# A hybrid attention block on one core: attention in two rounds over the heads, with the output projection and FFN products inside the second

## The chip, the core and the metric

The kernel runs on one core of a Trainium2 chip. The metric is the device time of one execution in microseconds (us). A core has five engines that the text names: PE (TensorE, matmuls and transpositions), DVE (VectorE) and ACT (ScalarE), which read the results of PE and prepare its operands, POOL (GpSimd), and SP, which issues the DMA transfers in one queue. Each engine works through its own list of instructions in the order of the program; semaphores tie the lists together. Operands lie in SBUF (128 partitions), results of PE in eight PSUM banks.

## What is computed

A decoder layer on one sequence of 1024 tokens and width 1024, in float32. The cut reference:

```
a = rmsnorm(h); q, k, v, u, z = split(a @ w_in)         # q, k, v, u, z: 1024 x 512
attn = dilated_attention(q, k, v)                       # 8 heads of 64, causal, windows
                                                        # (128, 1), (512, 4), (2048, 16), merged
sgu = spatial_gating(u, z)                              # chunks of 128 tokens
mixed = concat(rmsnorm(attn), rmsnorm(sgu)) @ w_out
h = h + rmsnorm(mixed)
f = rmsnorm(h)
g, up = split(f @ w_gate_up)                            # each 1024 x 2816
h = h + rmsnorm((silu(g) * up) @ w_down)
h = h + sigmoid(h @ w_pe_gate + b) * (p @ w_pe_proj)
```

## The kernel before

**Numbers.** Every large product is made of three matmuls (`mm3`): each operand is split (`split`) into a high half, which ACT casts, and a low half, which DVE subtracts; hi*hi, hi*lo and lo*hi are summed in a PSUM bank. A product of two matrices of 2 x 2 blocks is done as seven block products q = 1 to 7 instead of eight, in `ORDER` (1, 2, 6, 5, 7, 3, 4); the token side of these blocks is held, split, in a `Feat`. `Feat.first` takes the normed tiles 0 to 3 (128 tokens each), transposes them and `put`s blocks 1 and 2; `Feat.second` takes tiles 4 to 7 and forms the other five. Each `put` is two ACT copies and two DVE subtractions of 128 x 256.

**Stages.** The input product (v, then u and z, then q and k), attention, the output projection, the FFN and the gated embedding. Attention goes over four pairs of heads, `attention(pr)`. Each pair has five steps for each of its two heads: step 0 and 1 treat the first half of the queries, "far" the dilated blocks, 2 and 3 the second half; `merge` joins the parts. A step is a chain: score matmuls, a softmax on DVE and ACT, transpositions on PE, a split by ACT and DVE, products with v on PE, and a transposition back. `prepare(pr)` splits q and k of a pair and stacks their halves with nine copies from SBUF to SBUF, each from or to 64 partitions. Between the steps `feed` takes work from `others`, which does not hang on attention: `ple` (the products with `w_pe_proj`) and `gated` (the part of the output projection that takes `sgu`).

Behind attention, `rows_out(t)` does for a tile of 128 tokens the attention part of the output projection (`attn_out`) and the norms (`h_chain`); the normed tile goes to `F.first` or `F.second`. Between the calls of `F.second` the generator `ahead` is fed: `first_products(n)` does, for one of the 22 tiles n of the FFN's width, the two of the seven products (q = 1, 2) that need the first four tiles of tokens only. `gate_up(n)` does the rest of tile n, or all seven products. In the kernel before, `first_products` runs for n = 0 to 6, its results lie in SBUF.

**Order.** The program is recorded as a graph of operations (`Graph`), and `order()` sets the order of each engine by list scheduling: an operation's rank is its place in the recorded program, a ready operation of lower rank goes first, and an engine looks 80 (PE), 40 (DVE, ACT) or 12 (SP) waiting operations ahead. Tiles come from pools, `CAP`: 47 of 4 KB a partition (names m), 14 of 2 KB (s), 28 small ones (t) and the 8 PSUM banks (p); d is DRAM, c a constant. `limits` bounds some groups further: two PSUM banks for fillers ("fill"), three for scores, two for products with v ("av"). All instructions are issued by one line, L382 (L383 in the changed kernel), so that operations are told apart by their tiles.

## Time and profile before

| | us |
|---|---|
| median of three runs | 1205.39 (1204.2 to 1206.11) |
| the profiled execution | 1206.22 |
| its span, first to last instruction | 1204.4 |
| PE busy | 1179.1 (98%) |
| DVE busy | 840.7 (70%) |
| ACT busy | 585.6 (49%) |
| POOL busy | 82.4 (7%) |

The span is the time from the first to the last instruction; the profiled execution's time is a little longer. Busy times of one engine are summed over its instructions. The stages in this execution: the input products last until 226 us, attention from 226 to 461 (its last pair, with rows_out of the first four tiles, from 368), rows_out and the feature tiles of the FFN to 513, the first products to 608, `gate_up` to 894, and then the down product and the embedding.

### The profile page before, as it was taken

The numbers are of one execution on the slowest core, as the hardware profiler recorded it, in microseconds if no ns is written. First come the engines' busy times: TensorE is split into PE (matmuls) and PEld (weight loads), VectorE is DVE, ScalarE is ACT, GpSimd is POOL, SyncE is SP. The second block draws the span as 40 slices with busy tenths as digits, with TensorE's granted clock in tenths as the row PEclk, the third lists the DMA queues.
The fourth block names the chain that finished last, engine by engine and source line by source line (L and its number), as shares of the span: only waits on it lengthen the run. The fifth ranks groups of instructions, "written<-read, shape, count | busy, mean of one in ns | idle before, by whom it ended". The sixth has DMA issues, their size and how long they took to land.

```text
span 1204.4 us, 15994 instructions
## 1 busy us (share of the span) xinstructions
PE 1179.1 (98%) x5633; PEld 983.8 (82%) x5633; DVE 840.7 (70%) x1652; ACT 585.6 (49%) x1262; POOL 82.4 (7%) x124
## 2 busy tenths in 40 slices
PE   8999999999999999899999999999999999999998
PEld 6788888798888777788888888888888888888887
DVE  6888893278646889999865666656567965468643
ACT  7653333399868767632233333333344445357121
POOL 3101010001100244000000000000000000005000
PEclk9999999999999999999999999999999999999999
DMA  8224131859715245315433233233298323753111
GB/s 287 72 79 138 37 127 45 188 174 276 187 39 176 71 140 165 98 53 182 160 111 100 97 125 115 69 121 123 97 333 295 97 96 99 230 178 140 44 44 53
DMA packets 124554, 158.40 MB, mean 132 GB/s; under 512 B 9838, under 2 KB 72634, under 8 KB 124475
## 3 DMA queue, kind: packets, MB, share of 16 engines
q1 hardware_dynamic: 124474, 157.39, 41.0%
q8 instruction: 44, 0.72, 0.3%
q14 instruction: 36, 0.29, 0.1%
HBM read 108.83 MB, written 39.09 MB: 123 GB/s over the span
## 4 chain that ended last, share of the span: by engine, by line
PE 89%; ACT 4%; DVE 3%; POOL 1%; DMA 1%; issue 1%; SPq 0%; DVEq 0%; ACTq 0%; POOLq 0%
PE p L382 89%; ACT m L382 2%; ACT s L382 2%; DVE m L382 2%; POOL t L382 1%; DVE s L382 1%; DVE t L382 1%; DMA m<-in_x 0%; DMA m<-m 0%; SPq L382 0%; ACT t L382 0%; DVEq L382 0%; DVE c L382 0%; ACTq L382 0%; POOLq L382 0%
## 5 line engine op out<-in xcount | busy, mean ns | idle before, releaser
L382 PE MATMUL p<-m,m 128*128 128x512 f32 (+3 forms) x4620 | 1070.0, 390 | 12.4 <-DVE m L382 5.5
L382 PEld LDWEIGHTS p<-m,m 128*128 128x128 f32 x4620 | 861.7, 191 | 184.2 <-DVE m L382 7.2
L382 DVE TENSOR_TENSOR m<-m,m 128x512 fp32r<-128x512 f32 (+2 forms) x473 | 316.6, 704 | 97.7 <-ACT m L382 87.3
L382 ACT CAST m<-m 128x512 fp32r<-128x512 f32 x371 | 219.4, 624 | 246.4 <-PE p L382 158.1
L382 DVE TENSOR_TENSOR s<-p,s 128x512 f32<-128x512 f32 (+4 forms) x159 | 100.8, 642 | 112.5 <-PE p L382 69.5
L382 ACT COPY s<-p 128x512 f32<-128x512 f32 (+1 forms) x139 | 77.0, 557 | 82.4 <-PE p L382 78.9
L382 ACT ACTIVATE s<-s 128x512 f32<-128x512 f32 (+1 forms) x53 | 32.7, 623 | 128.7 <-DVE s L382 128.2
L382 DVE TENSOR_TENSOR m<-p,m 128x256 fp32r<-128x256 f32 (+3 forms) x141 | 67.0, 504 | 38.1 <-PE p L382 26.5
L382 POOL TENSOR_SCALAR t<-t 128x1 f32<-128x1 f32 (+1 forms) x56 | 22.4, 401 | 1009.4 <-ACT m L382 819.7
L382 ACT COPY m<-p 128x512 f32<-128x512 f32 (+1 forms) x85 | 38.7, 473 | 45.6 <-PE p L382 44.4
L382 ACT CAST m<-s 128x256 fp32r<-128x256 f32 (+1 forms) x105 | 47.3, 492 | 26.6 <-PE p L382 16.6
L382 DVE TENSOR_TENSOR m<-s,m 128x256 fp32r<-128x256 f32 (+1 forms) x105 | 51.9, 523 | 5.7 <-ACT m L382 5.7
L382 DVE TENSOR_TENSOR s<-s,s 128x512 f32<-128x512 f32 x75 | 51.1, 690 | 2.6 <-ACT s L382 0.7
L382 PE MATMUL p<-c,m 128*128 128x128 f32 x328 | 48.3, 274 | 0.7 <-DVE s L382 0.4
L382 ACT ACTIVATE m<-m 128x1024 f32<-128x1024 f32 (+2 forms) x45 | 42.5, 945 | 13.3 <-DVE m L382 8.5
L382 POOL TENSOR_TENSOR t<-t,c 128x1 f32<-128x1 f32 (+1 forms) x56 | 45.0, 804 | 4.7
L382 DVE TENSOR_TENSOR s<-p,m 128x512 f32<-128x512 f32 (+1 forms) x32 | 21.6, 674 | 33.5 <-PE p L382 33.1
L382 PE MATMUL p<-c,s 128*128 128x128 f32 (+2 forms) x249 | 42.1, 284 | 3.0 <-DVE s L382 2.8
L382 PEld LDWEIGHTS p<-c,m 128*128 128x128 f32 x328 | 38.0, 140 | 5.9 <-DVE s L382 1.0
L382 DVE CUSTOM_DVE_ANT_0 m<-p,m 128x384 f32<-128x384 f32 (+2 forms) x64 | 30.8, 502 | 15.5 <-PE p L382 15.4
L382 PEld LDWEIGHTS p<-c,s 128*128 128x128 f32 (+2 forms) x249 | 30.9, 146 | 12.4 <-DVE s L382 5.5
L382 ACT CAST s<-p 128x512 fp32r<-128x512 f32 (+2 forms) x64 | 32.5, 532 | 14.0 <-PE p L382 13.8
(58 smaller groups left out, 589.4 us busy)
## 6 DMA issues: line engine op xcount, KB each, us to landing
m<-d SPq DMA_DIRECT2D x55, 512.0 KB, 4.3
d<-s SPq DMA_DIRECT2D x104, 256.0 KB, 2.1
m<-in_w_gate_up SPq DMA_DIRECT2D x88, 256.0 KB, 4.1
m<-in_w_down SPq DMA_DIRECT2D x44, 256.0 KB, 6.1
m<-in_w_in SPq DMA_DIRECT2D x20, 512.0 KB, 4.6
m<-m SPq DMA_DIRECT2D x36, 256.0 KB, 5.0
m<-in_x SPq DMA_DIRECT2D x16, 512.0 KB, 6.0
s<-d SPq DMA_DIRECT2D x16, 256.0 KB, 5.1
```

Source lines behind the costliest of these rows:

```text
L382: getattr(getattr(nc, o.engine), o.what)(*[real(v) for v in o.args], **{k: real(v) for k, v in o.kw.items()})
```

## The change

q and k are kept in halves: the first halves (`qk_low`) stay in SBUF, the second halves, and k's first, are stored to DRAM as they are made (`qd`, `kd`). Attention runs in two rounds over the four pairs. Round one, `first_half`, does steps 0 and 1 of a pair; round two, `second_half`, does "far", 2, 3 and the merge, with q and k loaded again (`prepare_high`). v is loaded in halves, its split first half goes to DRAM in round one and comes back in round two; the biases are loaded once in each round. As the first 512 queries are complete after round one, `rows_out(0)` to `rows_out(3)` and `F.first` run inside round two's first pair, and `first_products` is a filler from then on. It runs for 20 tiles n instead of 7, and its results go to DRAM (`ed`) and are loaded again in `gate_up`. `Feat.second` forms a block and puts it, one after the other, in the order 6, 5, 7, 3, 4, with three small tiles instead of five. `order()` returns the operations in the order in which it picked them.

```diff
-        return sorted(ops, key=lambda o: (o.start, o.i))
+        return picked
...
-        def second(self, t, halves):
+        def second(self, t, halves, order=(6, 5, 7, 3, 4)):
...
-            ps = transposed(halves[0], 4)
-            copy(x3, ps)
-            tt(s3, x1, ps, SUB)
+            copy(x3, transposed(halves[0], 4))
             ps = transposed(halves[1], 4)
-            self.put(4, t, ps)
             tt(s1, ps, x3)
             tt(s2, s1, x1, SUB)
-            tt(s4, x2, s2, SUB)
-            for q, v in ((5, s1), (6, s2), (3, s4), (7, s3)):
-                self.put(q, t, v)
+            for q in order:
+                if q == 7:
+                    tt(x3, x1, x3, SUB)
+                if q == 3:
+                    tt(s2, x2, s2, SUB)
+                self.put(q, t, {6: s2, 5: s1, 7: x3, 3: s2, 4: ps}[q])
...
-    qf, kf = [M() for _ in range(4)], [M() for _ in range(4)]
+    qk_low, qk_high = [M(F32, (P, 2, 512)) for _ in range(4)], [M(F32, (P, 2, 512)) for _ in range(4)]
+    qd, kd = DR([AW, 512]), DR([AW, S])
...
+            if q in (3, 7, 4):
+                load({3: kd[rs, LO], 7: kd[rs, HI], 4: qd[rs]}[q], dst)
...
+    def stacked(q, k):
...
+        both, ql = M(F32R, (P, 2, 512)), SM(F32R)
+        qh, q1 = both[:, 0], both[:, 1]
...
+            split(kh[:, cs], kl[:, cs], v)
+        load(q1[bot].f32(), qh[bot].f32(), 0.6)
+        load(q1[top].f32(), ql[bot].f32(), 0.6)
+        load(qh[bot].f32(), ql[top].f32(), 0.6)
         for dst, src in ((k1, kh), (l1, kl)):
...
+            load(dst[bot].f32(), src[bot].f32(), 0.6)
+            load(dst[top].f32(), src[bot].f32(), 0.6)
+        load(kh[bot].f32(), kh[top].f32(), 0.6)
+        load(kl[bot].f32(), kl[top].f32(), 0.6)
+        return (qh, kh, kl), (q1, k1, l1)
+
+    def prepare_low(pr):
+        low = qk_low[pr]
+        qk[pr] = stacked(low[:, 0], [low[:, 1]])
+
+    def prepare_high(pr):
+        rs = slice(pr * P, (pr + 1) * P)
+        q, k = SM(), M()
+        load(q, qd[rs])
+        load(k, kd[rs])
+        qk[pr] = stacked(q, [k[:, LO], k[:, HI]])
...
+    EARLY = 20
+    FB, FH, FF2, FA, FO = 36, 0, 48, 60, 100
+    TODO = (((0, "far"), ("h", 0)), ((0, "far"), ("h", 1)), ((0, 2), ("h", 2)), ((0, 2), ("h", 3)), ((0, 3), ("f", 0)),
+            ((0, 3), ("f", 1)), ((0, 3), ("f", 2)), ((0, 3), ("f", 3)))
+    ed = {n: DR([2 * P, 512]) for n in range(EARLY)}
...
     def first_products(n):
 
-        both = M(F32, (P, 2, 512)) if n < 5 else None
-        p1, gate0 = early[n] = (both[:, 0], both[:, 1]) if both else (SM(), SM())
-        raw = M(F32, (P, 8, P), "raw")
+        p1, gate0, raw = SM(), SM(), M(F32, (P, 8, P), "raw")
...
         copy(p1, ps)
+        load(ed[n][:P], p1)
...
         tt(gate0, ps, p1)
+        load(ed[n][P:], gate0)
+        early.add(n)
...
     def gate_up(n):
...
-            (u, gate0), one, p1 = early.pop(n), PB(), None
-            p1, u = u, SM()
+            one, u, gate0, p1 = PB(), SM(), SM(), SM()
+            load(p1, ed[n][:P])
+            load(gate0, ed[n][P:])
...
+    def first_half(pr, fills, then):
+        v, b, vs, both = load_v(pr, slice(0, 512)), M(F32, (P, 2, 512)), [], M(F32R, (P, 8, P))
+        load(b, a["c_bias"][2 * pr : 2 * pr + 2, :, :512].rearrange("h p c -> p h c"))
         for hh in range(2):
...
+            v_halves(vhl, v, hh)
+            load(vcd[pr][hh].then(lambda u: u.rearrange("(j p) d -> p j d", p=P)), vhl.f32())
+            vs.append({j: vhl[:, j, :] for j in range(4)})
+        for step in (0, 1):
+            for hh in range(2):
+                unit(pr, hh, step, vs[hh], b[:, hh])
+                fed(fills, (0.15, 0.35)[step])
+            if step in then:
+                then[step]()
+
+    def second_half(pr, fills, then):
+        v, v3, vs, biases = load_v(pr, slice(512, S)), SM(F32R, (P, 2, P)), [], []
+        for hh in range(2):
+            b, vhl = M()[:, :896], M(F32R, (P, 8, P))
             load(b, a["c_bias"][2 * pr + hh])
+            load(vhl[:, :4, :].f32(), vcd[pr][hh].then(lambda u: u.rearrange("(s c) d -> s c d", c=4)))
+            load(v3[:, hh, :].f32(), vcd[pr][hh][384:512])
+            v_halves(vhl[:, 4:, :], v, hh)
...
-        for step in (0, 1, "far", 2, 3):
+        for step in ("far", 2, 3):
...
+                fed(fills, {"far": 0.15, 2: 0.12, 3: 0.23}[step])
...
-    prepare(0)
-    for pr in range(3):
-        attention(pr, [(others, (40, 60, 110)[pr])], {1: lambda: prepare(pr + 1)})
-    attention(3, [(others, 104)], {"far": lambda: rows_out(0, 1), 2: lambda: rows_out(2, 3)})
+    prepare_low(0)
+    for pr in range(4):
+        nxt = (lambda: prepare_low(pr + 1)) if pr < 3 else (lambda: prepare_high(0))
+        first_half(pr, [(others, FA)], {0: nxt})
+    ahead = chain(*(first_products(n) for n in range(EARLY)))
...
+    for pr in range(4):
+        then = {}
+        for step in ("far", 2, 3):
+            def hook(pr=pr, step=step):
+                for name, t in todo.get((pr, step), ()):
+                    if name == "h":
+                        rows_out(t)
+                    else:
+                        F.first(t, halves_of(t))
+                        if t == 3:
+                            fills.append((ahead, FB))
+                if step == 2 and pr < 3:
+                    prepare_high(pr + 1)
+            then[step] = hook
+        second_half(pr, fills, then)
     run(others)
-    ahead = chain(*(first_products(n) for n in range(7)))
-    for t in range(4):
-        rows_out(t + 4)
-        F.first(t, halves_of(t))
-    feed(ahead, 24)
     for t in range(4, NT):
-        feed(ahead, 24)
+        feed(ahead, FH)
+        rows_out(t)
+    for t in range(4, NT):
+        feed(ahead, FF2)
         F.second(t, halves_of(t))
     run(ahead)
```

How it moves instructions, at three places. First PE, where the products of q and k end. Before, the last product (q = 4, the split weights m_1988) is followed by transpositions and products of `ple` (c_73 is the identity, s_1772 a tile of p):

```order
L382 MATMUL p_1551<-m_527,m_1988 128x512
L382 MATMUL p_1551<-m_547,m_1988 128x512
L382 MATMUL p_1551<-m_527,m_1988 128x512
L382 MATMUL p_2158<-c_73,s_1772 128x128 x2
L382 MATMUL p_2161<-c_73,s_1859 128x128 x2
L382 MATMUL p_2173<-c_73,s_1990 128x128 x2
L382 MATMUL p_2178<-m_1835,s_2168 128x512
L382 MATMUL p_2178<-m_1897,s_2168 128x512
```

In the changed kernel the same product (weights m_2005) is followed by the first scores (m_2101 and m_2110 hold the stacked k of two heads, m_1773 their q):

```order
L383 MATMUL p_1565<-m_561,m_2005 128x512
L383 MATMUL p_1565<-m_577,m_2005 128x512
L383 MATMUL p_1565<-m_561,m_2005 128x512
L383 MATMUL p_2197<-m_2101,m_1773 128x128
L383 MATMUL p_2199<-m_2101,m_1773 128x256
L383 MATMUL p_2202<-c_73,s_1790 128x128 x2
L383 MATMUL p_2206<-m_2110,m_1773 128x128 x2
L383 MATMUL p_2209<-c_73,s_1830 128x128 x2
L383 MATMUL p_2217<-m_2110,m_1773 128x256 x2
L383 MATMUL p_2197<-m_2101,m_1773 128x128
```

The scores of the first pair have moved up to the last product, and the transpositions of `ple` stand between them.

Second DVE, near the end of `F.second`. Before (the `put`s have 128x2x128; the 128x512 rows with two m tiles as sources are splits of FFN weights):

```order
L382 TENSOR_TENSOR s_5725<-m_5199,s_5710 128x512
L382 TENSOR_TENSOR m_5468<-s_5700,m_5456 128x2x128
L382 TENSOR_TENSOR m_5475<-s_5700,m_5461 128x2x128
L382 TENSOR_TENSOR m_5481<-s_5710,m_5464 128x2x128
L382 TENSOR_TENSOR m_5489<-s_5710,m_5470 128x2x128
L382 TENSOR_TENSOR m_5507<-s_5725,m_5473 128x2x128
L382 TENSOR_TENSOR m_5519<-s_5725,m_5479 128x2x128
L382 TENSOR_TENSOR m_5527<-s_5673,m_5431 128x2x128
L382 TENSOR_TENSOR m_5541<-s_5673,m_5437 128x2x128
L382 TENSOR_TENSOR m_5533<-m_5386,m_5533 128x512
L382 TENSOR_TENSOR m_5646<-m_5386,m_5646 128x512
```

And in the changed kernel:

```order
L383 TENSOR_TENSOR m_6008<-s_5908,m_5992 128x2x128
L383 TENSOR_TENSOR m_6013<-s_5908,m_5995 128x2x128
L383 TENSOR_TENSOR s_5939<-m_4177,s_5939 128x512
L383 TENSOR_TENSOR m_5898<-m_5786,m_5898 128x512
L383 TENSOR_TENSOR m_5982<-m_5850,m_5982 128x512
L383 TENSOR_TENSOR m_6041<-s_5939,m_6029 128x2x128
L383 TENSOR_TENSOR s_6046<-p_6010,s_6015 128x512
L383 TENSOR_TENSOR m_6006<-m_5850,m_6006 128x512
L383 TENSOR_TENSOR s_6066<-p_6048,s_6051 128x512
L383 TENSOR_TENSOR m_6071<-s_5939,m_6033 128x2x128
```

The run of eight `put` subtractions ahead of a split is gone; splits stand between the `put`s.

Third SP, in `gate_up`. Before, loads of raw weights (m from in_w_gate_up) and stores of results (d from s or m):

```order
L382 DMA d_98<-m_5449 128x512
L382 DMA m_6131<-in_w_gate_up 128x4x128 x2
L382 DMA d_99<-m_5554 128x512
L382 DMA d_100<-s_6220 128x512
L382 DMA d_101<-s_6235 128x512
L382 DMA d_102<-s_6120 128x512
L382 DMA d_103<-s_6253 128x512
L382 DMA m_6267<-in_w_gate_up 128x4x128
```

In the changed kernel, at a similar place, with the first products' results coming back (s from d_102, d_103):

```order
L383 DMA m_6454<-in_w_gate_up 128x4x128 x2
L383 DMA m_6461<-in_w_gate_up 128x4x128 x2
L383 DMA s_6474<-d_102 128x512
L383 DMA d_119<-s_6471 128x512
L383 DMA s_6483<-d_102 128x512
L383 DMA d_119<-s_6500 128x512
L383 DMA m_6570<-in_w_gate_up 128x4x128 x2
L383 DMA m_6579<-in_w_gate_up 128x4x128 x2
L383 DMA s_6592<-d_103 128x512
L383 DMA d_120<-s_6081 128x512
```

Between the weight loads stand the reloads of `ed`, each 128x512.

## Rows read from the trace of the kernel before

**Rows 1.** The page, part 1: busy us (share of the span) and instructions of each engine.

```profile
PE 1179.1 (98%) x5633; PEld 983.8 (82%) x5633; DVE 840.7 (70%) x1652; ACT 585.6 (49%) x1262; POOL 82.4 (7%) x124
```

**Rows 2.** Table by stretches; its first line names the columns, x counts instructions.

```profile
core 0: us, PE busy (x) PEld busy (x) DVE busy (x) ACT busy (x) POOL busy (x), PEclk, DMA share, GB/s
226.00:247.00 21.00, 18.07 (x93) 15.49 (x92) 8.83 (x35) 13.38 (x34) 0.00 (x0) 0.92 0.88 233
247.00:368.00 121.00, 120.85 (x751) 105.78 (x749) 79.09 (x261) 100.89 (x282) 6.83 (x16) 1.00 0.61 173
368.00:461.00 93.00, 87.27 (x500) 73.13 (x499) 79.62 (x194) 72.55 (x197) 25.06 (x41) 1.00 0.36 116
461.00:513.00 52.00, 48.17 (x221) 39.45 (x220) 47.19 (x91) 33.85 (x79) 9.81 (x11) 0.97 0.46 132
513.00:608.00 95.00, 95.00 (x420) 78.69 (x420) 85.51 (x134) 28.50 (x47) 0.00 (x0) 1.00 0.43 136
608.00:894.00 286.00, 286.00 (x1263) 236.89 (x1262) 170.41 (x262) 101.45 (x180) 0.00 (x0) 1.00 0.36 119
```

**Rows 3.** Timeline of PE, 225 to 247 us: start, length, instruction xcount [idle before <-releaser].

```profile
226.12 0.81 PE L382 MATMUL p<-c,s 128*128 128x128 f32 x6
...
234.71 2.39 PE L382 MATMUL p<-m,m 128*128 128x128 f32 x8 [2.57 <-DMA m<-m]
...
242.48 0.82 PE L382 MATMUL p<-c,m 128*128 128x128 f32 x6
...
246.03 0.66 PE L382 MATMUL p<-s,m 128*128 128x256 f32 x4
```

**Rows 4.** PE by form in the four stretches, in turn: xcount | busy, mean ns | idle before.

```profile
L382 PE MATMUL p<-m,s 128*128 128x512 f32 x30 | 8.1, 426 | 0.4 <-ACT s L382 0.4
...
L382 PE MATMUL p<-m,m 128*128 128x512 f32 x6 | 2.3, 476 | 0.0
...
L382 PE MATMUL p<-m,m 128*128 128x512 f32 x190 | 55.5, 411 | 0.0
...
L382 PE MATMUL p<-m,s 128*128 128x512 f32 x66 | 21.6, 421 | 0.0
...
L382 PE MATMUL p<-m,m 128*128 128x512 f32 x203 | 51.3, 398 | 3.0 <-ACT m L382 2.6 <-DVE t L382 0.2
...
L382 PE MATMUL p<-m,m 128*128 128x512 f32 x189 | 46.2, 403 | 3.8 <-DVE m L382 3.8
```

**Rows 5.** Waits of PE, 226 to 513 us: releaser, us in total, times, longest us.

```profile
PE p L382 <- DVE m L382: 3.8, 1, 3.8
PE p L382 <- ACT m L382: 2.6, 2, 1.4
PE p L382 <- DMA m<-m: 2.6, 1, 2.6
```

**Rows 6.** Timeline of PE, 496 to 517 us.

```profile
506.99 10.31 PE L382 MATMUL p<-m,m 128*128 128x512 f32 x37 [3.83 <-DVE m L382]
```

**Rows 7.** Timeline of DVE, 503 to 509 us.

```profile
503.57 2.77 DVE L382 TENSOR_TENSOR m<-s,m 128x256 fp32r<-128x256 f32 x8
506.25 1.89 DVE L382 TENSOR_TENSOR m<-m,m 128x512 fp32r<-128x512 f32 x3
...
508.17 0.69 DVE L382 TENSOR_TENSOR m<-m 128x512 f32<-128x512 f32 x1
```

**Rows 8.** Timeline of SP's issues, 214 to 240 us.

```profile
214.76 15.76 SPq L382 DMA_DIRECT2D m<-m  x14
```

**Rows 9.** DMA issues by kind: xcount, KB each, median us from issue to landing.

```profile
d<-s SPq DMA_DIRECT2D x104, 256.0 KB, 2.1
m<-in_w_gate_up SPq DMA_DIRECT2D x88, 256.0 KB, 4.1
...
m<-m SPq DMA_DIRECT2D x36, 256.0 KB, 5.0
...
s<-d SPq DMA_DIRECT2D x16, 256.0 KB, 5.1
```

**Rows 10.** DVE by form, 226 to 513 us: xcount | busy, mean ns | idle before, releaser.

```profile
L382 DVE TENSOR_TENSOR s<-p,s 128x512 fp32r<-128x512 f32 x32 | 22.0, 689 | 17.8 <-ACT s L382 17.5
```

More of the change, by code (lines that the diff above doesn't have):

```diff
@@ L246, in order @@
         coming, events = [], [0.0]
-        done, first = [False] * n, 0
+        done, first, picked = [False] * n, 0, []
         def release(o):
@@ L321, in order @@
                 o.start, o.engine = now, e
+                picked.append(o)
                 if o.table and o.table != table:
@@ L630, in x_chain @@
             norm_apply(v, xt[:, cs], rstd, g_pre[:, cs])
-        (A.first if t < 4 else A.second)(t, xn)
+        (A.first if t < 4 else A.second)(t, xn, *([(4, 5, 6, 3, 7)] if t >= 4 else []))
     def v_out(t, terms):
@@ L886, in far_unit @@
         oT = SM()
-        copy(oT.then(lambda v: v.rearrange("p (s c) -> p c s", c=4)), po)
-        turn_back(oT, far[pr][:, :, hh * HD : (hh + 1) * HD], 4)
+        copy(oT.split(4), po.then(lambda v: v.rearrange("p c s -> p s c")))
+        turn_back(lambda ii: oT[:, ii * P : (ii + 1) * P], far[pr][:, :, hh * HD : (hh + 1) * HD], 4)
     def merge(pr):
@@ L993, in h_chain @@
         kept[t] = m
-    raws, early, y_even = {}, {}, []
+    raws, early, y_even = {}, set(), []
     def halves_of(t):
@@ L1086, in feed, with v_halves, load_v @@
             n -= got
-    def attention(pr, fills, then):
-        v = M(F32, (P, 8, P))
-        load(v, vd[:, pr * P : (pr + 1) * P].then(lambda x: x.rearrange("(j p) c -> p j c", p=P)))
-        biases, vhls = [], []
-        for hh in range(2):
-            b = M()[:, :896]
+    vcd = [[DR([512, P]) for _ in range(2)] for _ in range(4)]
+    def v_halves(dst, v, hh):
+        split(dst[:, :, 0:HD], dst[:, :, HD:], v[:, :, hh * HD : (hh + 1) * HD])
+    def load_v(pr, rs):
+        v = SM(F32, (P, 4, P))
+        load(v, vd[rs, pr * P : (pr + 1) * P].then(lambda x: x.rearrange("(j p) c -> p j c", p=P)))
+        return v
@@ new lines, in fed @@
+    def fed(fills, share):
+        for fill, n in fills:
+            feed(fill, n * share)
+    def first_half(pr, fills, then):
+        v, b, vs, both = load_v(pr, slice(0, 512)), M(F32, (P, 2, 512)), [], M(F32R, (P, 8, P))
+        load(b, a["c_bias"][2 * pr : 2 * pr + 2, :, :512].rearrange("h p c -> p h c"))
+        for hh in range(2):
+            vhl = both[:, 4 * hh : 4 * hh + 4, :]
+            v_halves(vhl, v, hh)
[7 more added lines that the diff above has]
+                then[step]()
@@ L1097, in attention @@
-            split(vhl[:, :, 0:HD], vhl[:, :, HD:], v[:, :, hh * HD : (hh + 1) * HD])
-            vhls.append(vhl)
-        vcs = []
-        for vhl in vhls:
-            vcd, vc = DR([512, P]), SM(F32R, (P, 4, P))
-            load(vcd.then(lambda u: u.rearrange("(j p) d -> p j d", p=P)), vhl[:, :4, :].f32())
-            load(vc.f32(), vcd.then(lambda u: u.rearrange("(s c) d -> s c d", c=4)))
-            vcs.append(vc)
+            vs.append({3: v3[:, hh, :], "far": vhl[:, :4, :], **{j: vhl[:, j, :] for j in range(4, 8)}})
@@ L1105, in attention @@
         stats[pr], far[pr] = [T1(8) for _ in range(4)], SM(F32, (P, 4, P))
-        for step in (0, 1, "far", 2, 3):
+        for step in ("far", 2, 3):
             for hh in range(2):
                 if step == "far":
-                    far_unit(pr, hh, vcs[hh], biases[hh])
+                    far_unit(pr, hh, vs[hh]["far"], biases[hh])
                 else:
-                    unit(pr, hh, step, vhls[hh], biases[hh])
-                for fill, share in fills:
-                    feed(fill, share * {0: 3, 1: 7, "far": 5, 2: 4, 3: 7}[step] / 52.0)
+                    unit(pr, hh, step, vs[hh], biases[hh])
+                fed(fills, {"far": 0.15, 2: 0.12, 3: 0.23}[step])
```

54 lines of the change are left out of this document (25 added, 29 removed).

## Prediction

> **What bounds the kernel now.** I read the page's busy shares first: TensorE (PE) is busy 98% of the span, VectorE (DVE) 70%, ScalarE (ACT) 49% [rows 1]. PE is the bound, and neither kernel saves it work: the order of the changed kernel holds the same 5601 PE instructions. So the only time to win is time in which PE stands still or steps slowly. The table by stretches tells where that is [rows 2]: from 513 to 894 us PE is busy 95.00 of 95.00 and 286.00 of 286.00 us; the gaps lie between 226 and 513 us, in attention (226 to 461) and in the norms and feature products behind it (461 to 513).
>
> Busy time hides part of it, since PE overlaps its matmuls: a 512-column matmul has a mean of some 400 ns [rows 4], but 1263 of them fill 286.00 us, so one starts every 0.2264 us [rows 2]. Short ones start every 0.11 us (128 columns: 0.82 us for six, (0.82 − 0.27)/5) to 0.12 us (256 columns: (0.66 − 0.30)/3) [rows 3]; I take 0.113 for all of them. Now each stretch gets a floor, its 512-column matmuls [rows 4] by 0.2264 plus the rest by 0.113, and a slack, its length less that floor:
>
> 226 to 247: 36 and 57, floor 14.6, slack 6.4. 247 to 368: 256 and 495, floor 113.9, slack 7.1 (6% of the floor). 368 to 461: 203 and 297, floor 79.5, slack 13.5 (17%). 461 to 513: 189 and 32, floor 46.4, slack 5.6 (12%). Sum: 254.4 of floor, **32.6 us of slack**.
>
> Why it is there: the first stretch has one wait of 2.57 us on the copies that stack q and k, and then a granted clock of 0.92 on average [rows 2, 3, 5]. The two levels being 1 and 1/2, that is (1 − 0.92) × 2 × 21 = 3.4 us at the lower one, 1.7 us lost. The last has one wait of 3.83 us: a split (the subtraction that makes the low half of a weight tile) stands on DVE behind eight `put` subtractions, 2.77 us, of `F.second` [rows 6, 7]; the clock after it costs (1 − 0.97) × 52 = 1.6 us [rows 2]. The two middle ones have many small gaps. What separates 6% from 17% there is load. DVE's busy time against the floor is 79.6/79.5 = 1.00 in 368 to 461 and 47.2/46.4 = 1.02 in 461 to 513, against 79.1/113.9 = 0.69 (ACT 0.89) in 247 to 368; from 513 to 608 it is 85.5/95 = 0.90, and PE does not stop [rows 2]. So gaps grow when DVE's load reaches PE's.
>
> The Trainium skill ("Perfetto Trace Analysis", section Identifying the Most-Contended Engine) says that the busy share of matmuls is not a good measure of the distance to the roof, and that the share of weight loads (LDWEIGHTS) is. The rows bear out the first half: the matmuls leave only 287 − 274.4 = 12.6 us idle in 226 to 513, far less than the slack. The second half decides a rival below.
>
> **The change, part by part.** Nothing is removed from PE. What moves is work that does not hang on attention: 13 more n of `first_products` (n 7 to 19, 24 matmuls each, 312 × 0.2264 = 70.6 us) go from `gate_up` to the stretch around attention, 216 matmuls of n 0 to 8 inside round two, and rows_out and `F.first` of the first four tiles go into round two as well. I cut the changed PE order into stages, counted its matmuls, put DVE's and ACT's instructions of each stage at the durations of the trace, and gave each stage the slack of the nearest row by load:
>
> (a) Start of attention, 143 matmuls (64 long), floor 23.4, load DVE 0.71, ACT 0.91. The low halves of k are done 48 matmuls (10.9 us) before the first score, since q=4 only writes the second half of q. But 16 DMAs stand ahead on SP's queue (the stores of k, the copies of pairs 0 and 1), which now move at 0.5 to 1.13 us each (14 copies took 15.76 us [rows 8]; half as long ones should take half). 16 × 0.65 = 10.4 us: the scores wait for 0 to 2 us. And no `ple` work stands behind q=4 to fill it. I take 3 us, between nothing and the 6.4 of today.
> (b) Rest of round one, 485 (240), floor 82.0, loads 0.54 and 0.76: below those of 247 to 368, so 6% as there, 4.9.
> (c) rows_out 0 to 3 and `F.first` in pair 0, 274 (100), floor 42.3, DVE 0.96, ACT 0.85: nearly the 1.00 of 368 to 461, so 15%, 6.3.
> (d) Pairs 1 to 3 with FFN products, 547 (228), floor 87.7, loads 0.73 and 0.74: 6%, 5.3.
> (e) rows_out 4 to 7, 171 (144), floor 35.7, DVE 0.80: between 0% (at 0.90, 513 to 608) and 17%, I take 8%, 2.9.
> (f) `F.second` with 216 long matmuls of FFN products between its tiles, floor 52.5, DVE 0.89: like 513 to 608, 0.5. Two things take the wait at 503 away: `put` subtractions alternate with the splits in DVE's order, and there are two n of ready products (48 matmuls, 10.9 us) for each tile, against 2.77 us of subtractions.
> (g) `gate_up` of 20 early n. Each of the 13 new ones turns two ACT copies into DVE additions and adds a third: 39 × 0.60 us ((1.89 − 0.69)/2 for a 512-column one [rows 7]) = 23.4 us of DVE, its load there rising from 0.60 to 0.80, below the 0.90 that cost PE nothing. It adds 40 reloads of 256 KB. A reload lands in 5.1 us and a raw weight tile in 4.1 [rows 9], and the order issues them a whole n (60 matmuls, 13.6 us) ahead. I take 1 us.
>
> Floors of (a) to (f) sum to 323.6 = 254.4 + 70.6 less rounding, so no PE work is lost in the count. Slacks: 3 + 4.9 + 6.3 + 5.3 + 2.9 + 0.5 + 1 = 23.9 against 32.6, **a gain of 8.7 us**. The profiled run took 1206.22 us, its span 1204.4; 1206.22 − 8.7 = 1197.5. That run lies 0.83 above the median of 1205.39, so the median should be **1196.7**.
>
> Bounds. (b) and (d) could be at 17% (+9.0, +9.6) or at none (−4.9, −5.3), (a) at 6.4 or 0, (c) at 6 to 17% (−3.7, +0.9), (e) at 0 or 17% (−2.9, +3.2), (f) at up to 5.6 (+5.1), (g) at up to 4 (+3.0). All highs together are not likely: as independent ends their squares sum to a width of 15 up and 9.5 down. Since the loads of (b) and (d) are below that of the 6% row, their upper ends are remote, and I take two thirds of the upward width.
>
> **Rivals.** *Nearly no gap is left:* with FFN products at hand in (c) to (f) PE never starves, as from 513 to 608. Then (c) to (f) fall to some 2 us, (b) to 3, in all 9 to 10 with (a) and (g): 1205.39 − 23 = 1182. Against it: round one has only the same fillers as today, and each product needs a split of its own on the loaded DVE.
>
> *The gaps move along:* they are the latency of score, softmax, transposition, split, product. DVE stands for 17.5 us in 226 to 513 behind ACT's casts in that chain [rows 10], and the change has as many of these chains as before. Slack then stays at some 30: 1203 to 1205, no change.
> Read by the weight loads, as that page has it, there is little to win: 233.85 of 287 us is 81.5% in 226 to 513 against 82.8% in 608 to 894, room for 4.6 us, and some 1201 at best; how far the trace bears this out is weighed in this rival's chance.
>
> *The copies become the bound (slower):* every hand-over of a pair in round two needs nine copies on 64 partitions, six of 1.13 us and three of half of that, 8.5 us of SP's queue, behind two loads from DRAM, with FFN loads and stores in the same queue. Copied bytes rise from 9.4 to 12.6 MB. In the order the last copy of pairs 1 to 3 is issued 42 to 49 PE rows (7 to 9 us) ahead of its use, and a copy lands in 5.0 us [rows 9]. If the queue is late by more than that, each hand-over costs what 231.8 us does today: 2.6 of wait and 1.7 of clock [rows 2, 3], 4.3 us; four of them are 17.2, hence 1196.7 + 17.2 = 1213.9. It decides from (1207.8 − 1196.7)/4 = 2.8 us a hand-over.
> By the skill ("SBUF — State Buffer", Door 1: The DMA port swizzle), transfers on 64 partitions reach half of the ports, some 218 GB/s; fourteen copies in 15.76 us are 233 GB/s [rows 8], which agrees. By that rule, which speaks against this change, 3.1 MB more would be an estimated 14 us of port time; it costs only where PE waits for it.
>
> That the change does not do what it says is excluded: the order shows the two rounds, and the FFN products among them.
>
> **How the numbers follow.** Forecast (gaps partly closed) 0.68, nearly no gap 0.09, gaps move along 0.12, copies 0.11. Range: 1186 (the forecast's lower width of 9.5, and a part of the second case beyond) to 1206 (two thirds of 15 upwards, with most of the no-change case). A measurement can tell about 0.2% (2.4 us) from no change: faster is below 1203.0, slower above 1207.8. Faster takes nearly all of the forecast and the second case: 0.76; same 0.13; slower 0.11.
>
> **What would show it.** Right: the 2.57 and 3.83 us waits of PE are gone, the clock is 1.00 where `F.second` runs, and PE's busy share is near full from the FFN products on. (a) wrong: PE waits for copies at the first scores. (c) wrong: a stretch with rows_out in pair 0 whose DVE is full and whose PE idles by more than 7 us. (g) wrong: PE waits on DVE or on reloads in `gate_up`. The prediction fails if several waits on copies of over 2 us, each with a fall of the clock, appear between pairs of round two, or if DVE bounds two of the stages.

## The result and the profile after

The changed kernel takes 1194.29 us (median, 1191.19 to 1200.4), the kernel before 1205.39: 11 us faster. The ratio, here and below taken from the means of the runs, is 0.9914, with a 95% interval of 0.9891 to 0.9937. The forecast was 1196.7, with a range of 1186 to 1206. The execution that was profiled took 1197.43 us, its span 1195.6; against the 1206.22 us of the profiled execution before that is 8.8 us less (forecast: 8.7). So the sum holds in both ways of counting, but most of its terms do not, and that is where the learning is.

The page, part 1, as in [rows 1]: PE is the bound as before, DVE has 28 us more to do, ACT 15 us less.

```profile
PE 1175.6 (98%) x5633; PEld 981.4 (82%) x5633; DVE 868.5 (73%) x1702; ACT 571.0 (48%) x1248; POOL 83.6 (7%) x125
```

The table by stretches, in the columns of [rows 2], cut at the borders of the stages (a) to (g) of the prediction; (a) begins at 223.40 us, and 348.0 us lie behind (g):

```profile
223.40:247.20 23.80, 23.80 (x145) 20.73 (x144) 17.08 (x52) 22.91 (x61) 0.00 (x0) 1.00 0.99 323
247.20:333.20 86.00, 85.55 (x486) 73.27 (x485) 48.34 (x139) 66.40 (x175) 8.98 (x24) 1.00 0.66 207
333.20:383.70 50.50, 47.04 (x275) 40.34 (x275) 40.84 (x107) 36.65 (x102) 14.77 (x19) 1.00 0.57 165
383.70:485.10 101.40, 97.48 (x548) 83.78 (x549) 65.96 (x200) 67.46 (x192) 0.00 (x0) 0.97 0.71 199
485.10:521.10 36.00, 36.00 (x172) 29.85 (x171) 28.89 (x50) 18.57 (x41) 15.30 (x23) 1.00 0.41 131
521.10:573.60 52.50, 52.50 (x249) 43.90 (x248) 48.29 (x93) 34.05 (x78) 3.40 (x3) 1.00 0.81 259
573.60:847.60 274.00, 272.72 (x1202) 225.07 (x1202) 229.14 (x356) 76.18 (x134) 0.00 (x0) 1.00 0.55 170
```

Taking the prediction's floors from these lengths gives the slack of each stage:

| stage | length | floor | slack forecast | slack measured |
|---|---|---|---|---|
| (a) start of attention | 23.8 | 23.4 | 3 | 0.4 |
| (b) rest of round one | 86.0 | 82.0 | 4.9 | 4.0 |
| (c) pair 0 of round two, rows_out, F.first | 50.5 | 42.3 | 6.3 | 8.2 |
| (d) pairs 1 to 3 with FFN products | 101.4 | 87.7 | 5.3 | 13.7 |
| (e) rows_out 4 to 7 | 36.0 | 35.7 | 2.9 | 0.3 |
| (f) F.second with FFN products | 52.5 | 52.5 | 0.5 | 0.0 |
| (g) gate_up, 20 n | 274.0 | 271.7 | 1 | 2.3 |
| sum | 624.2 | 595.3 | 23.9 | 28.9 |

In whole lengths: 226 to 894 us before [rows 2] was 668.0; two n of `gate_up` (2 x 84 matmuls x 0.2264 = 38.0 us) now lie behind (g), so 630.0 stand against 624.2, 5.8 us won. The part ahead is 2.6 us shorter (226.0 to 223.4), the part behind 0.4 (310.4 to 348.0 − 38.0): 8.8. By the slacks only 32.6 − 28.9 = 3.7 of the 5.8 would be won. The other 2.1 us are in the floors: a row by stretches counts a matmul that lies across a border in both stretches. The counts before hold 7 long and 5 short matmuls more than those of (a) to (g) (2199 against 2192, 881 against 876), though the work is the same, and 7 x 0.2264 + 5 x 0.113 = 2.1 us. Counted once, the slack before is 34.7 us, and 5.8 us of it are won.

PE's waits between 223 and 574 us, as in [rows 5]: the 3.8 us behind the `put`s are gone, and so is the copy at 231.8 us, but another copy is waited for.

```profile
PE p L383 <- DMA m<-m: 2.4, 1, 2.4
PE p L383 <- DVE m L383: 2.2, 2, 1.4
...
```

That one is at the hand-over to the last pair. PE's timeline, and the table by stretches around it:

```profile
446.83 1.06 PE L383 MATMUL p<-m,m 128*128 128x512 f32 x4
450.29 1.19 PE L383 MATMUL p<-m,m 128*128 128x128 f32 x4 [2.40 <-DMA m<-m]
```

```profile
440.00:450.00 10.00, 7.89 (x49) 6.70 (x47) 2.87 (x8) 5.10 (x14) 0.00 (x0) 1.00 1.00 249
450.00:455.00 5.00, 4.71 (x19) 4.41 (x20) 3.96 (x17) 3.14 (x7) 0.00 (x0) 0.77 0.69 228
455.00:460.00 5.00, 5.00 (x24) 4.30 (x23) 2.77 (x13) 3.28 (x14) 0.00 (x0) 0.89 0.05 20
```

The reader is to see three things: PE waits 2.40 us; the DMA engines were busy throughout the 10 us ahead (share 1.00) and yet moved no more than 249 GB/s, where stage (a) moved 323 at 0.99; and the clock fell behind the wait, to 0.77 and 0.89, which costs 0.23 x 5 + 0.11 x 5 = 1.7 us. What fills these 10 us is not the copies. The DMA view of the stretch:

```profile
DMA packets 3327, 2.49 MB, mean 249 GB/s; under 512 B 95, under 2 KB 3001, under 8 KB 3326
...
m<-in_w_gate_up SPq DMA_DIRECT2D x2, 512.0 KB, 9.9
...
m<-m SPq DMA_DIRECT2D x1, 256.0 KB, 10.2
```

One copy of 256 KB is issued there. It lands 10.2 us later, beside two raw weight tiles of 512 KB, and nine of ten packets are under 2 KB. So the copy landed late in a queue full of other transfers, here loads of the FFN products that the change pulled into the stage. That these loads alone make it late is not shown: e4, which has none of them in round two, also waits 1.6 us for a copy at a hand-over. Copies alone are seen before, in the 14 of [rows 8]:

```profile
214.80:230.60 15.80, 15.43 (x71) 12.56 (x70) 4.92 (x9) 5.46 (x12) 0.00 (x0) 1.00 0.92 200
```

The Trainium skill ("SBUF — State Buffer", Door 1: The DMA port swizzle) puts transfers on 64 partitions at half of the ports, some 218 GB/s; this row, 200 GB/s at a share of 0.92, agrees. (The prediction's 233 GB/s divides by the time of issuing, in which the last copies had not yet landed.)

The stage (c) has its waits where DVE and ACT are both full. Two rows of the table by stretches:

```profile
380.00:385.00 5.00, 2.79 (x13) 1.83 (x14) 5.00 (x13) 5.00 (x19) 0.00 (x0) 0.95 1.00 258
385.00:390.00 5.00, 5.00 (x23) 4.25 (x23) 3.23 (x10) 3.25 (x13) 0.00 (x0) 0.71 0.65 227
```

From 380 to 385 us DVE and ACT are busy for 5.00 of 5.00, PE for 2.79; the clock is 0.95 and then 0.71, another 0.25 + 1.45 = 1.7 us, all of it in (d), as the clock is 1.00 to the end of (c) at 383.7 us.

The third place in (d) is a raw weight tile that comes late. ACT, then PE:

```profile
414.89 0.62 ACT L383 CAST m<-m 128x512 fp32r<-128x512 f32 x1 [1.82 <-DMA m<-in_w_gate_up]
```

```profile
415.83 0.44 PE L383 MATMUL p<-c,s 128*128 128x128 f32 x2 [1.40 <-ACT s L383]
```

ACT stands 1.82 us for `m<-in_w_gate_up`; behind it in ACT's list stands a copy for attention, and PE waits 1.40 us for that with a transposition.

### The profile page after: what moved, and what is told of

It is laid out like the page before. It is cut to its first block, busy times and chain, and to the rows that moved or that the text cites. A ratio compares the mean times of both kernels' runs of the same rounds, so it can differ in the third digit from the quotient of the medians.

```text
span 1195.6 us, 16385 instructions
## 1 busy us (share of the span) xinstructions
PE 1175.6 (98%) x5633; PEld 981.4 (82%) x5633; DVE 868.5 (73%) x1702; ACT 571.0 (48%) x1248; POOL 83.6 (7%) x125
## 4 chain that ended last, share of the span: by engine, by line
PE 89%; DVE 3%; DMA 3%; ACT 2%; POOL 1%; issue 1%; SPq 0%; ACTq 0%; DVEq 0%; POOLq 0%
PE p L383 89%; DVE s L383 2%; ACT m L383 2%; POOL t L383 1%; DMA s<-d 1%; DMA m<-m 1%; DVE t L383 1%; DVE m L383 1%; DMA m<-in_w_gate_up 1%; DMA m<-in_w_in 1%; ACT s L383 0%; POOL m L383 0%; SPq L383 0%; ACTq L383 0%; DVEq L383 0%
## 5 line engine op out<-in xcount | busy, mean ns | idle before, releaser
L383 DVE TENSOR_TENSOR s<-p,s 128x512 f32<-128x512 f32 (+4 forms) x218 | 139.3, 653 | 79.6 <-PE p L383 49.6
L383 ACT ACTIVATE s<-s 128x512 f32<-128x512 f32 (+1 forms) x71 | 44.1, 626 | 227.6 <-DVE s L383 171.7
L383 DVE TENSOR_TENSOR m<-p,m 128x256 fp32r<-128x256 f32 (+3 forms) x136 | 63.7, 496 | 44.4 <-PE p L383 23.4
L383 ACT COPY s<-p 128x512 f32<-128x512 f32 (+1 forms) x118 | 59.9, 516 | 47.2 <-PE p L383 46.4
L383 ACT CAST m<-s 128x256 fp32r<-128x256 f32 (+1 forms) x121 | 53.1, 478 | 35.4 <-DMA s<-d 12.5
L383 DVE TENSOR_TENSOR s<-s,s 128x512 f32<-128x512 f32 x88 | 60.7, 692 | 4.4 <-ACT s L383 0.7
L383 ACT ACTIVATE m<-m 128x1024 f32<-128x1024 f32 (+1 forms) x36 | 36.8, 1023 | 31.2 <-DVE m L383 16.9
L383 PE MATMUL p<-s,m 128*128 128x128 f32 (+1 forms) x256 | 45.8, 284 | 0.2 <-PE p L383 0.2
L383 PEld LDWEIGHTS p<-s,m 128*128 128x128 f32 x256 | 39.9, 197 | 4.4 <-ACT m L383 0.4
L383 ACT ACTIVATE m<-m,t 128x384 f32<-128x384 f32 (+2 forms) x64 | 37.1, 583 | 8.6 <-DVE t L383 8.5
```

The source lines that it names most:

```text
L383: getattr(getattr(nc, o.engine), o.what)(*[real(v) for v in o.args], **{k: real(v) for k, v in o.kw.items()})
```

## The experiments

Each is compared with the kernel before on the same chip; the ratio is given with its interval. Two parts were first taken one by one.

**e1: the new F.second alone, in the kernel before** (with the order of picking; F.second also serves the input products, there in the order 4, 5, 6, 3, 7 as in the changed kernel).

```diff
-        def second(self, t, halves):
+        def second(self, t, halves, order=(6, 5, 7, 3, 4)):
...
-        return sorted(ops, key=lambda o: (o.start, o.i))
+        return picked
```

> The kernel before with the new Feat.second alone (a block is formed and put, one after the other; x_chain with its own order 4, 5, 6, 3, 7) and the order of picking; attention in one round, seven n of first products as before. Theory 'puts': the gain is made where PE is 2.6 us earlier at the start of attention (226.0 against 223.4 us) and where the 3.83 us wait behind eight put subtractions went with its clock (5.6 us of slack in 461 to 513 against 0.3 in the two stages of after); two rounds win some 9 us in round one and lose as much in round two. Then this kernel takes 1205.4 - 2.6 - 5 = 1198. Theory 'products at hand': the gain comes from 13 more n to fill gaps, and the start is an accident: 1203 to 1205.

Measured: 1203.42 us, 0.9991 (0.9981 to 1.0002): no difference that can be told. The wait has shrunk by 0.9 us only. DVE and then PE, around 500 us:

```profile
497.60 0.42 DVE L383 TENSOR_TENSOR m<-p,m 128x256 fp32r<-128x256 f32 x1
...
498.60 1.76 DVE L383 TENSOR_TENSOR m<-s,m 128x256 fp32r<-128x256 f32 x5
500.27 1.29 DVE L383 TENSOR_TENSOR s<-m,s 128x512 f32<-128x512 f32 x2
501.48 0.68 DVE L383 TENSOR_TENSOR m<-m,m 128x512 fp32r<-128x512 f32 x1
```

```profile
502.22 58.11 PE L383 MATMUL p<-m,m 128*128 128x512 f32 x248 [2.97 <-DVE m L383]
```

The split (the 128x512 `m<-m,m`) stands behind eight `put` subtractions as before, three from 497.60 us on and the five shown, and behind two sums, and PE waits 2.97 us instead of 3.83. So at this place the `put`s do not alternate with splits; the new F.second does not bring that about by itself. Theory 'puts' falls.

**e2: 20 n of first products through DRAM as well, attention still in one round.**

```diff
-    ahead = chain(*(first_products(n) for n in range(7)))
+    ahead = chain(*(first_products(n) for n in range(EARLY)))
...
-    feed(ahead, 24)
     for t in range(4, NT):
-        feed(ahead, 24)
+        feed(ahead, FF2)
```

> The same, and 20 n of first products through DRAM, 48 matmuls of them ahead of each tile of F.second; attention still in one round. Theory 'puts': the wait is gone already, so no more than 1 us against the kernel with the new puts alone, 1197 to 1199; and as two rounds bring nothing, equal to the changed kernel within 3 us. Theory 'products at hand': as the gaps of 368 to 513 lie where products can't yet help in one round, 1199 to 1202, and the two rounds make the rest.

Measured: 1202.42 us, 0.9986 (0.9977 to 0.9995). The wait in F.second is gone with 48 matmuls between its tiles, but some of it comes back in `gate_up`, where the kernel before has none. PE's waits, 600 to 900 us:

```profile
PE p L383 <- DVE s L383: 2.4, 2, 1.7
```

So products without the two rounds are worth some 1.7 us, less than either theory gave.

**e3: the changed kernel with 7 n of first products.**

```diff
-    EARLY = 20
+    EARLY = 7
```

> The changed kernel with 7 n of first products instead of 20 (through DRAM as there). They are used up in round two's second and third pair and nothing is left for F.second. Theory 'products at hand': F.second starves as before, 4 to 8 us more than the changed kernel, 1199 to 1202. Theory 'puts': the puts alternate with nothing to split, F.second costs PE 2 us at most, and gate_up is rid of 26 reloads: 1192 to 1196.

Measured: 1228.56 us, 1.0194 (1.0169 to 1.0219). Slower than the kernel before by 23 us, and the changed kernel by 34, far beyond either expectation. The seven n are used up, and F.second stands alone. The row for its stretch:

```profile
505.00:536.00 31.00, 8.28 (x38) 6.12 (x37) 29.94 (x57) 18.86 (x50) 10.13 (x9) 0.60 0.56 170
```

DVE is busy 29.94 of 31 us, PE 8.28, and the clock is 0.60.

**e4: the changed kernel without first products in round two** (all 20 n remain, fed from F.second on).

```diff
-    FB, FH, FF2, FA, FO = 36, 0, 48, 60, 100
+    FB, FH, FF2, FA, FO = 0, 0, 48, 60, 100
```

> The changed kernel with no first products inside round two (all are fed from F.second on). Theory 'products at hand': pairs 1 to 3 of round two lose their filler, and 216 matmuls (49 us) of cover with it; slack there grows from 13.7 to 20 or more: 1200 to 1206. Rival 'queue': the slack in round two is made by transfers (at 440 to 450 us the DMA engines are busy 1.00 and PE waits 2.4 us for a stacking copy), and with nine fewer raw loads of 512 KB in the queue the wait goes: 1190 to 1194.

Measured: 1209.43 us, 1.0042 (1.0027 to 1.0057): 5 us slower than before, 15 slower than the changed kernel. The gaps open in round two, and the clock goes with them:

```profile
384.00:410.00 26.00, 21.92 (x126) 18.25 (x124) 22.59 (x76) 23.19 (x76) 0.00 (x0) 0.87 0.76 217
410.00:450.00 40.00, 35.44 (x226) 31.50 (x227) 29.32 (x107) 30.68 (x97) 0.00 (x0) 0.91 0.56 154
```

PE's idle time in these rows, 4.1 and 4.6 us, is only half of the price: the clock takes up to 0.13 x 26 + 0.09 x 40 = 7.0 us more. (From 384 to 450 us the changed kernel has 3.6 us of idle time and 1.7 of clock.) Theory 'products at hand' stands: two rounds without products inside them cost time, products without the two rounds (e2) hardly save any, both together are 10 to 11 us faster.

**e8: 24 matmuls instead of 48 between the tiles of F.second.**

```diff
-    FB, FH, FF2, FA, FO = 36, 0, 48, 60, 100
+    FB, FH, FF2, FA, FO = 36, 0, 24, 60, 100
```

> The changed kernel with 24 instead of 48 matmuls of first products ahead of each tile of F.second (the rest follows behind it). The stage's matmuls shrink from 52.5 to some 31 us, DVE's work there from 48 to some 40: DVE's load goes from 0.9 to 1.3 of PE's. Theory 'load': DVE becomes the bound of the stage, 6 to 10 us more: 1200 to 1205. Rival: it needs only something at hand between the tiles, as the puts alternate with splits: 1194 to 1197.

Measured: 1212.35 us, 1.006 (1.0042 to 1.0077), 17.6 us above the changed kernel (0.0146 x 1205), the sign of theory 'load' with a larger size. The stage, and then PE's wait behind it:

```profile
521.00:541.00 20.00, 19.98 (x101) 16.48 (x99) 19.82 (x39) 15.18 (x40) 4.24 (x4) 1.00 0.84 263
541.00:550.00 9.00, 0.04 (x1) 0.04 (x1) 8.68 (x22) 7.06 (x18) 0.00 (x0) 0.61 0.35 115
```

```profile
549.96 12.28 PE L383 MATMUL p<-m,m 128*128 128x512 f32 x46 [8.98 <-DVE m L383]
```

DVE is busy 19.82 of 20.00 and 8.68 of 9.00 us. Once the products run out PE stands 8.98 us while DVE works off its `put`s, and the clock falls behind that (0.84 in the following 10 us, 1.6 us lost). That is 10.6 of the 14.1 us by which the span is longer (1209.7 against 1195.6); where the others lie was not traced to a place. So (f) costs nothing only because 48 matmuls a tile keep DVE's load below PE's; 24 do not, and none (e3) makes DVE the bound of the whole stage.

**e7: every stacking copy issued twice**, in both rounds (72 transfers more, of the same data).

```diff
         load(q1[bot].f32(), qh[bot].f32(), 0.6)
+        load(q1[bot].f32(), qh[bot].f32(), 0.6)
...
```

> The changed kernel with each of the nine stacking copies issued twice, in both rounds: 72 more transfers, some 4.5 us more of SP's queue for a pair in round one and 8.5 us in round two. Theory 'queue at its limit': the copies land 7 to 9 us ahead of use at best, so every hand-over of round two comes 4 to 8 us late and takes the clock with it: 1210 to 1230. Rival 'covered': the fillers and the other head's work cover it, at most one wait more: 1194 to 1200.

Measured: 1208.77 us, 1.0034 (1.0022 to 1.0045): 14.5 us above the changed kernel (0.0120 x 1205), just under what 'queue at its limit' gave and far above 'covered'. But the hand-overs do not come late one by one, as that theory had it: in the whole run PE waits for a copy once, for 1.2 us, and mostly for ACT. Two of PE's waits, the longest of them, the table around it, and an issue of SP:

```profile
PE p L383 <- ACT s L383: 7.4, 5, 3.9
...
PE p L383 <- DMA m<-m: 1.2, 1, 1.2
```

```profile
466.36 0.96 PE L383 MATMUL p<-c,s 128*128 128x128 f32 x2 [3.89 <-ACT s L383]
```

```profile
462.00:467.00 5.00, 1.10 (x7) 0.58 (x5) 4.12 (x23) 1.44 (x7) 0.00 (x0) 0.85 1.11 290
467.00:475.00 8.00, 7.65 (x29) 6.70 (x30) 5.81 (x15) 6.11 (x16) 0.00 (x0) 0.50 1.02 281
```

```profile
461.62 3.92 SPq L383 DMA_DIRECT2D m<-in_w_gate_up  x3
```

The wait shows as one on ACT, at the end of a softmax; the DMA engines are full during it and behind it (shares of 1.11 and 1.02). No FFN product stands beside that softmax, and raw weight tiles are issued at 461.62 us, just ahead of the wait. So the doubled copies most likely cost time by making the loads of the fillers late; no run tests that. A wait of 3.89 us is followed by 8 us at half clock, 4 us more.

**e5: the stacking of the next pair one step earlier.**

```diff
-                if step == 2 and pr < 3:
+                if step == "far" and pr < 3:
                     prepare_high(pr + 1)
```

> The changed kernel with prepare_high(pr + 1) called one step earlier (after 'far' instead of after step 2). In the changed kernel PE waits 2.40 us at 450 us for a stacking copy of the last pair, with the DMA engines busy 1.00 from 440 to 450 us, and the clock costs some 1.7 us after it. Theory 'queue': issued a step (about 10 us) earlier the copies are there, the wait and its clock go: 3 to 4 us less, 1190 to 1192 on the scale where the changed kernel has 1194.3. Rival: the transfers are served in one queue, so what is earlier for one is later for the raw weights of the products; the wait turns up at a split: 1193 to 1197.

Measured: 1193.47 us, 0.9906 (0.989 to 0.9923). The wait on copies is gone from the list of PE's waits, 223 to 574 us, which begins as shown, and from 440 to 460 us PE does not stop and the clock is 1.00:

```profile
PE p L383 <- DVE m L383: 1.6, 2, 0.9
...
```

```profile
440.00:460.00 20.00, 20.00 (x118) 17.46 (x117) 15.15 (x50) 13.44 (x42) 0.00 (x0) 1.00 0.61 186
```

What was expected of the place came; of the 3 to 4 us, about 1 us shows against the changed kernel's 0.9914, which lies within both intervals.

**e9: the changed kernel once more.**

> The changed kernel itself once more, as the measure for the two beside it on the same chip: 1191 to 1198, ratio to the kernel before 0.989 to 0.994.

Measured: 1196.0 us, 0.9921 (0.9908 to 0.9935). The hand-over to the last pair waits here too, but shorter, so this term varies between executions:

```profile
PE p L383 <- DMA m<-m: 1.4, 1, 1.4
```

**e10 and e11: other shares of fillers, with the earlier hook.**

```diff
-    FB, FH, FF2, FA, FO = 36, 0, 48, 60, 100
+    FB, FH, FF2, FA, FO = 36, 0, 48, 48, 100
```

> prepare_high one step earlier, and 48 instead of 60 matmuls of ple and gated for a pair in round one, so that some 48 more of them are left for round two's first pair, where rows_out 0 to 3 and F.first stand. Theory 'load': PE has 8 us of gaps there because DVE's work is as long as PE's; 48 matmuls (10.9 us) more beside it, with less than half as much DVE work, cover a part: 2 to 4 us less than with the earlier hook alone, 1189 to 1192. Rival: round one (DVE load 0.54, ACT 0.76) lives on those fillers and opens as much: 1193 to 1196.

```diff
-    FB, FH, FF2, FA, FO = 36, 0, 48, 60, 100
+    FB, FH, FF2, FA, FO = 48, 0, 48, 60, 100
```

> prepare_high one step earlier, and 48 instead of 36 matmuls of first products for a pair from the last F.first on: 12 n inside round two instead of 9, 8 for F.second, none behind it. Theory 'products at hand': the gaps of pairs 1 to 3 (some 8 us with the earlier hook) shrink by 2 to 4 us: 1189 to 1192. Rival 'queue': three more raw loads of 512 KB and six more stores in the queue of round two make copies or raws late: 1195 to 1200.

Measured: 1193.6 us, 0.9901 (0.9888 to 0.9915), and 1192.32 us, 0.9895 (0.9879 to 0.991). Neither tells anything of its theory: `feed` rounds up to whole steps of the generator, and at 48 the steps are as many as at 60 and at 36, so that both were the program of e5. They are repeats of it: 0.9906, 0.9901, 0.9895, against 0.9914 and 0.9921 of the changed kernel. On this evidence the earlier hook is worth 0.1 to 0.25%, 1 to 3 us.

**e6: rows_out and F.first of the first four tiles spread over one and a half pairs.**

```diff
-    TODO = (((0, "far"), ("h", 0)), ((0, "far"), ("h", 1)), ((0, 2), ("h", 2)), ((0, 2), ("h", 3)), ((0, 3), ("f", 0)),
-            ((0, 3), ("f", 1)), ((0, 3), ("f", 2)), ((0, 3), ("f", 3)))
+    TODO = (((0, "far"), ("h", 0)), ((0, 2), ("h", 1)), ((0, 3), ("h", 2)), ((1, "far"), ("h", 3)), ((0, 3), ("f", 0)),
+            ((0, 3), ("f", 1)), ((1, "far"), ("f", 2)), ((1, 2), ("f", 3)))
```

> The changed kernel with rows_out 0 to 3 and F.first 0 to 3 spread over one and a half pairs instead of one (0, 1, 2 and the first two F.first within pair 0; 3 and the others within pair 1). In the changed kernel the stretch 333 to 384 us has 8.2 us of slack, DVE's list standing without a gap from 373 to 388. Theory 'load': DVE's load of 0.96 there makes the gaps, spread out they shrink to 4 us: 1190 to 1193. Rival 'products at hand': the first products can begin only after the last F.first, so pair 1 loses its filler, and the gaps move there: 1196 to 1202.

Measured: 1197.04 us, 0.9932 (0.9917 to 0.9947), in the range of the rival; the interval overlaps that of the changed kernel, so the spreading brought nothing, and whether it costs stays open. The trace shows why it brought nothing. Pair 0, and then a stretch of pair 1:

```profile
333.00:384.00 51.00, 50.91 (x301) 45.14 (x301) 38.38 (x109) 36.48 (x108) 13.96 (x19) 0.97 0.37 116
385.00:395.00 10.00, 5.80 (x33) 4.15 (x32) 9.11 (x25) 9.69 (x29) 3.11 (x3) 0.93 1.07 324
```

In pair 0 PE is idle for 0.1 us, against 3.5 in stage (c) of the changed kernel. In pair 1 it is idle for 4.2 of 10 us, where DVE and ACT are nearly full again. The DMA engines are full there too (1.07), but no wait of PE there ends on a transfer. So the gaps go with the load of DVE and ACT, and they went along with the work.

**e12: fewer fillers in round one, with the earlier hook.**

```diff
-    FB, FH, FF2, FA, FO = 36, 0, 48, 60, 100
+    FB, FH, FF2, FA, FO = 36, 0, 48, 40, 100
```

> prepare_high one step earlier, and a share of 40 instead of 60 for the fillers of round one. feed rounds up to whole steps of the generator (7 matmuls of ple, 12 of gated), so that 60 and 48 both give five steps for a head and use up all 32 in the fourth pair of round one, and the run with 48 was the same program as the one with 60 (as the run with 48 first products was the one with 36: three steps for a head in both). 40 gives three steps for a head: 24 in round one, 8 of gated (96 matmuls, 21.7 us) are left for round two's first pair, where PE has 9.3 us of slack between 360 and 390 us beside a full DVE. Theory 'load': they cover 3 to 5 us of it, 1188 to 1191. Rival: they bring their own splits and one more DVE operation each into the list that is full, and round one has a filler less for each step: 1192 to 1197.

Measured: 1191.48 us, 0.9883 (0.9866 to 0.9899), between the two ranges that were expected and the lowest of all; its interval lies below that of e9 (0.9908 to 0.9935), and overlaps those of e5, e10 and e11. By the ratios it is some 4 us below the changed kernel. That the fillers cover the gaps of pair 0 is not shown. The stretch that holds most of (c), in e5 and then in e12:

```profile
350.00:400.00 50.00, 46.55 (x260) 40.06 (x258) 41.14 (x105) 38.31 (x103) 10.62 (x16) 0.93 0.57 163
```

```profile
350.00:400.00 50.00, 47.37 (x256) 40.13 (x254) 37.27 (x95) 34.67 (x95) 7.91 (x11) 0.90 0.63 178
```

From 350 to 400 us PE is busy 47.37 us instead of 46.55, at a clock of 0.90 instead of 0.93. The gaps of (c) are still there.

## Why the prediction was right, and where it was not

**The sum.** The direction was right, and so was the idea: work that does not hang on attention, put where PE starved, saves time. e2, e3 and e4 show that it takes both halves of the change. That 8.7 us were forecast and 8.8 measured is luck. Only 5.8 of the 8.8 were won in the stages that the sum is about; 2.6 came ahead of them, where it had nothing, and 0.4 behind. And within the stages the terms missed on both sides: (a), (e) and (f) were to fall from 12.0 us of slack to 6.4 and fell to 0.7, while (b) to (d) were to fall from 20.6 to 16.5 and rose to 25.9.

**What the slack was made of.** A part of it is no gap at all. The prediction prices every short matmul at 0.113 us. The scores (128 columns, `p<-m,m`) are slower. Their row before, from 247 to 368 us, and eight of them in the changed kernel, at full clock:

```profile
L382 PE MATMUL p<-m,m 128*128 128x128 f32 x43 | 11.8, 394 | 0.0
```

```profile
458.25 2.09 PE L383 MATMUL p<-m,m 128*128 128x128 f32 x8
```

One begins every (2.09 − 0.39)/7 = 0.24 us. By that, an estimate, 43 scores hold 43 x 0.13 = 5.6 of the 7.1 us of slack in 247 to 368, where PE is idle for only 0.15 us [rows 2]. So the 6% that the prediction took from there is mostly the pace of the scores, not gaps that go with load, and no filler wins it. What fillers can win is idle time and clock. Before, these were 12.6 + 3.3 = 15.9 us in 226 to 513; in (a) to (g) they are 9.1 + 3.4 = 12.5, which is 3.4 of the 5.8 us won. The 10.1 us at the two ends (226 to 247 and 461 to 513) went to nothing in (a), (e) and (f); 247 to 461 had 5.9 us, and (b) to (d) have 11.2; (g) has 1.3. The other 2.4 of the 5.8 us lie in the pace of a PE that does not stop; their cause stays open.

**The start, not in the sum.** The 2.6 us ahead of attention were not forecast ("unchanged" was the silent assumption). Two runs of one program (e10 and e11) show how much chance there is. The last products with the first score, e10 and then e11:

```profile
222.14 3.34 PE L383 MATMUL p<-m,m 128*128 128x512 f32 x15
```

```profile
222.12 1.52 PE L383 MATMUL p<-m,m 128*128 128x512 f32 x7
```

They end at 225.48 and 223.64 us, 1.8 us apart, without any change of the program; in the kernel before the products end at 226.28. So up to 1.8 of the 2.6 us may be chance, not gain, and how much of the rest is gain stays open, as the kernel before was traced once.

**(a)** was too dear by 2.6 us. The step that failed is "16 x 0.65 = 10.4 us: the scores wait for 0 to 2 us": the row 223.40 to 247.20 has PE busy for all of its 23.80 us. The 2.57 us wait of [rows 3] and its clock went.

**(b)** 4.9 against 4.0: right in size but not for the reason given, as PE is idle for 0.45 us of the stage. **(f)** 0.5 against 0.0: right, with the products at hand as the reason, as e8 shows from the other side. Its other reason, `put`s that alternate with splits, is not borne out as a cause of its own: with the new F.second alone (e1) PE still waits 2.97 us, and the `put`s do not alternate there. It is the 48 matmuls that cover DVE. **(e)** 2.9 against 0.3: the value between 0% and 17% was too high.

**(c)** 6.3 against 8.2: the mechanism is right, DVE and ACT both full (e6 shows the gaps going with their load), the size was somewhat low. PE is idle for 3.5 us of it.

**(d)** is the term that was mis-sized: 5.3 forecast, 13.7 measured. The step that failed is "loads 0.73 and 0.74: 6%". The load was right (DVE 65.96/87.7 = 0.75), but it was not what set the gaps here: the copy that came late (2.4 + 1.7 us of clock), the clock that (c) left behind (1.7 us) and the raw weight that came late (1.4 us) are 7.2 us. The remaining 6.5 are hardly gaps, as PE is idle for 3.9 us in all and 3.8 of them are the two waits; they are a busy PE's pace, as in (b). The rows of 247 to 368 us, from which I took the 6%, had no loads of FFN weights beside the copies; the rule had no term for the queue.

**(g)** 1 against 2.3, within its bounds. Its sign of being wrong did show, once, where the kernel before has no wait:

```profile
775.34 4.83 PE L383 MATMUL p<-m,m 128*128 128x512 f32 x20 [1.28 <-DVE s L383]
```

**The rivals.** *The copies become the bound* was half there: one of the hand-overs came late in the profiled execution, at the price that was given (4.1 us against 4.3). e5 shows that a step of lead removes it, and e7 that more copies cost 14.5 us, though not by late hand-overs. *The gaps move along* did not decide, but it holds for the middle: the waits of [rows 3, 6] are gone, while idle time and clock went from 5.9 us in 247 to 461 to 11.2 in (b) to (d). The share of weight loads had given room for 4.6 us, and the 5.8 us won from (a) to (g) are more. The Trainium skill ("Perfetto Trace Analysis", section Identifying the Most-Contended Engine) names that share as a measure of the distance to the roof. That 82.8%, the share from 608 to 894 us, is the most that a stretch of attention can reach was the prediction's own step, and it failed: in (a), where PE does not stop, the share is 20.73/23.80 = 87%. *Nearly no gap is left* needed (c) and (d) at a few us.

## What to carry to other kernels

A stage in which the bound engine starves is cured by work that is ready and needs little of the engine that holds it up; count both engines' work in the new stage, since half the filler (e8) or none (e3) can cost more than the whole change brings. Before a slack is called a gap, price each kind of matmul by its own pace, and look for idle time and clock. When independent work is pulled into a stage, its transfers come with it: look for queue and DMA share, not for engine load alone, and give the hand-overs a step more of lead. Waits of PE can cost its clock as well, here between 40% (1.6 us after 3.83) and the full length of the wait (4 us after 3.89); which of the shorter ones do is not told by their length, as the next section shows.
